# Strassen's seven products in all columns of a down projection, with two weight sums per column made by accumulating loads

## The chip, the cores and the metric

The kernel runs on one core of a Trainium2 chip. The metric is device time in microseconds (us) of one execution. Engines are called as the profile calls them: PE (matrix products; PEld is its weight load), DVE (VectorE), ACT (ScalarE), POOL (GpSimd), SP (SyncE, which only issues DMAs here). All of them run their own instructions in the order in which the program wrote them.

## The reference, cut to what matters

One encoder block on 256 positions with 2048 features, in float32. The last part, in which the change lies, is the feed-forward half:

```python
def _conv_ffn(h, w_up, dw_w, dw_b, w_down):
    up = h @ w_up                                   # 2048 -> 2 x 5504
    gate, val = up[..., :D_FF], up[..., D_FF:]
    gate = conv_general_dilated(gate, dw_w, ...) + dw_b   # width 3, along the positions
    act = jax.nn.gelu(gate, approximate=False) * val
    return act @ w_down                             # 5504 -> 2048
```

Ahead of it stand a norm, an input projection, attention and a Fourier mixing, an output projection and a second norm; behind it the residual sum and a last norm.

## The kernel before, in words

**Operands in two parts.** Every matrix operand is split into a high part in a reduced float32 format (`hi`, a copy by ACT) and the rest (`lo`, a subtraction by DVE, lines 162 and 163, 894 and 895). A product of two such operands is hi x hi + hi x lo + lo x hi on PE. Weights come in tiles of 128 x 2048 numbers (1 MB), by DMAs that SP issues.

**Items.** The 5504 inner features are 43 tiles of 128. PE's work from the second norm on is a list of items (`ff_items`, line 62). An *up item*, `gate` or `val` of one tile, is 16 pairs of matmuls. Tiles 0 to 31 form four groups of eight; a group's down projection runs while the up items of the next group go on. `PATTERN` (line 59) gives the order of a group's items: u is an up item, d a plain down item, s a product. The eleven tiles from 32 on are multiplied afterwards (`down` and `last`).

**The group's down projection.** A group's activations are 1024 features by 256 positions, cut into 2 x 2 blocks (two halves of the features k, two of the positions t). The output columns are four blocks of 512. For the blocks 1 and 3 it is done plainly: four *plain items* with the weight blocks a, c, b, d, of 24 matmuls each (two position halves, 12 each). For the blocks 0 and 2 it is done by Strassen's scheme in Winograd's form: seven *products* P1, N5, N3, P7, P6, P2, N4 of 12 matmuls in place of eight. Their left operands are blocks of activations or sums of them (`operand`, `operand_sums`, lines 857 to 871); their right operands are weight blocks or sums of them: a, x = a+b, d, b+d, x+d, c, x+c. These four sums are DVE additions of 128 x 2048 (lines 912, 920, 927, 936) in the tile `sumw` or in b's own buffer. Each product is added to one or two outputs (`product_out`), and what several outputs share is gathered in three tiles `z_U`, `z_N5`, `z_P7`, and given out once after the last group (`shared_out`, lines 1012 to 1019).

**What sets the order.** Line by line, `ff_step(n)` (line 960) runs after PE's item n was written: first what is noted `beside` n (for the item before: copies and additions out of PSUM, the convolution, the product with the gate), then `split_item(n+2)`, the split of the weights of the item after next, and if the item is an up item one of the `pending` weight sums, then what is noted `behind` n (the GELU, the operands). So ACT and DVE have two items of lead over PE at most; `hi` and `lo` have three buffers each. The weights of the down projection come through a ring of two buffers (`ring_load`, line 880). The operands of the next group are noted at fixed distances after the group's last val item (lines 979 to 985).

**Late tiles.** The up items that go with group 3 are those of the tiles 32 to 39. Their activations are not gathered for a group but split at once (`val_mult`, lines 830 to 833): DVE multiplies, ACT makes the high half, DVE the low half.

Of the kernel before, what the change touches and what calls it, by code (L numbers as in the profile page):

```python
# [8 lines left out]
F32 = mybir.dt.float32  # L9
# [4 lines left out]
P = 128  # L14
# [44 lines left out]
PATTERN = "uuududdudsuusuusuusuusususu"  # L59


def ff_items():
# [20 lines left out]
def block_kernel(  # L83
# [36 lines left out]
    for n, it in enumerate(items):  # L120
        if it[0] in ("product", "plain"):
            continue
# [698 lines left out]
    def val_mult(j):  # L821
        va, ge = sums_of.pop(f"v{j}"), gate_out.pop(j)
        g, q = divmod(j, 8)
        if j >= 8 * N_GROUPS:
            if q % 2 == 0 or j == LAST[0]:
                tag = ("va", "va", "op_P1", "op_A10", "op_P7", "op_N5")[(j - 32) // 2]
# [23 lines left out]
    PLACE = {"P1": (0, 0), "A10": (0, 1), "P2": (1, 0), "N4": (1, 1)}  # L850
# [14 lines left out]
    def operand_sums(g):  # L865
        a00, a10, a01, a11 = (block_of(g, n) for n in ("P1", "A10", "P2", "N4"))
# [11 lines left out]
    ring_next = [0]  # L878

    def ring_load():  # L880
        if ring_next[0] < len(ring):
            key = ring[ring_next[0]]
            ring_next[0] += 1
            t = ring_tiles[key] = fp.tile([P, 2048], F32, tag="rawd", name="rawd%s%d%s" % key)
            col = 0 if key[0] == "s" else 1
            nc.sync.dma_start(t, w_down[(key[1] * 2 + col) * 4 + "abcd".index(key[2])])
# [3 lines left out]
    def two_parts(key, src):  # L890
        hi = wp.tile([P, 2048], F32R, tag="hi", name=f"hi_{key}", bufs=3)
        lo = wp.tile([P, 2048], F32R, tag="lo", name=f"lo_{key}", bufs=3)
        halves[key] = (hi, lo)
        nc.scalar.activation(hi, src, AF.Copy)
        nc.vector.tensor_tensor(lo, src, f32(hi), ALU.subtract)

    def split_product(g, p):
        key = ("product", g, p)
        name = f"{p}_{g}"
        tt = nc.vector.tensor_tensor  # L900
        raw = {w: ring_tiles.get(("s", g, w)) for w in "abcd"}

        def parts_of(src):
            two_parts(name, src)
            halves[key] = halves.pop(name)

        if p == "P1":
            parts_of(raw["a"])
            x = ring_tiles["x"] = fp.tile([P, 2048], F32, tag="sumw", name=f"sumw{g}", bufs=1)
# [6 lines left out]
        elif p in ("N5", "P6", "N4"):  # L916
            parts_of(ring_tiles["x"])
        elif p == "N3":
            parts_of(raw["d"])
# [381 lines left out]
```

## Time and profile before

| | |
|---|---|
| median of 3 runs | 980.5 us (979.66 to 981.6) |
| the profiled execution | 980.02 us, span 978.2 us, mean granted PE clock 0.996 |
| busy: PE, DVE, ACT, POOL | 968.0, 741.8, 516.7, 23.6 us |
| matmuls in one group of items | 180 in plain items and products, 512 in up items |
| moved by DMA | 186.41 MB |
| a weight tile of 1 MB from HBM, from issue to landing | 4.8 us (median) |

In the profile a row of a timeline gives the start, the duration, the engine, the line, the operation, what it writes and reads, and in brackets how long the engine was idle just before and what released it. A matmul's duration covers its way through the array, and the next starts long before its end; so PE's pace is read from start to start. A DVE instruction too starts some 0.08 us before the one ahead of it ends.

### The profile page before, as it was taken

To read this page: it belongs to the slowest core of one execution; us is meant where nothing else is said; L and a number is where in the kernel's file an instruction comes from. 1 tells how busy PE (TensorE), PEld (TensorE's weight loads), DVE (VectorE), ACT (ScalarE), POOL (GpSimd) and SP (SyncE) were. 2 spreads that over 40 slices of the span, in tenths; PEclk is the share of its full clock that TensorE was granted. 3 is DMA by queue.
4 is the path that set the end of the run, shared out by engine and by line. 5 is a ranking of instruction groups with operands and counts; after the bars stand their busy time and mean duration, and the time that the engine had idled before them with its cause. 6 is when DMAs were issued, how large, how long until landed. Compare 5 with 4: busy or idle time off the path is not lost.

```text
span 978.2 us, 12804 instructions
## 1 busy us (share of the span) xinstructions
PE 968.0 (99%) x5137; PEld 829.7 (85%) x5137; DVE 741.8 (76%) x923; ACT 516.7 (53%) x645; POOL 23.6 (2%) x35
## 2 busy tenths in 40 slices
PE   9999999999999999999999999999999999999996
PEld 7788898888888888888888888888888888888885
DVE  6658877576666668787887888778888878887765
ACT  6756766554454455455455455545555545543534
POOL 0000000000000000000000000000000000000003
PEclk9999999999999999999999999999999999999998
DMA  9854444445545755445554464645546544555532
GB/s 328 330 192 145 166 142 160 148 164 208 195 171 190 262 192 191 172 173 216 215 184 172 166 253 166 222 172 179 208 192 217 194 173 144 200 205 211 188 129 86
DMA packets 30091, 186.41 MB, mean 191 GB/s; under 512 B 3408, under 2 KB 3920, under 8 KB 9040
## 3 DMA queue, kind: packets, MB, share of 16 engines
q1 hardware_dynamic: 29744, 184.54, 51.9%
q8 instruction: 40, 0.66, 0.3%
q0 software_dynamic: 144, 1.05, 0.3%
q14 instruction: 19, 0.16, 0.0%
q10 hardware_dynamic: 144, 0.01, 0.0%
HBM read 183.49 MB, written 2.10 MB: 190 GB/s over the span
## 4 chain that ended last, share of the span: by engine, by line
PE 93%; DVE 4%; ACT 2%; DMA 1%; issue 0%; SPq 0%; POOL 0%; ACTq 0%; POOLq 0%
PE ps_val L312 15%; PE ps_gate L312 15%; PE ps_val L313 8%; PE ps_gate L313 8%; PE ps_q L312 5%; PE ps_q L313 2%; PE ps_a L303 2%; PE ps_a L302 2%; PE ps_a L301 2%; DVE lo L163 2%; PE ps_k L312 2%; PE ps_l L302 1%; PE ps_l L301 1%; PE ps_l L303 1%; PE ps_P L1028 1%; PE ps_P L1027 1%
## 5 line engine op out<-in xcount | busy, mean ns | idle before, releaser
L163 DVE TENSOR_TENSOR lo<-raw,hi 128x2048 fp32r<-128x2048 f32 (+3 forms) x146 | 315.3, 2159 | 90.1 <-ACT hi L162 90.0
L162 ACT ACTIVATE hi<-raw 128x2048 fp32r<-128x2048 f32 (+3 forms) x145 | 263.0, 1814 | 62.3 <-PE ps_l L302 18.4
L312 PE MATMUL ps_val<-hU,hi 128*128 128x512 f32 x688 | 242.9, 394 | 0.0
L312 PE MATMUL ps_gate<-hU,hi 128*128 128x512 f32 x688 | 242.8, 394 | 0.0
L313 PE MATMUL ps_val<-hU,lo 128*128 128x256 f32 x688 | 193.1, 281 | 0.1
L313 PE MATMUL ps_gate<-hU,lo 128*128 128x256 f32 x688 | 193.1, 281 | 0.0
L312 PEld LDWEIGHTS ps_gate<-hU,hi 128*128 128x128 f32 x688 | 129.4, 188 | 30.1
L312 PEld LDWEIGHTS ps_val<-hU,hi 128*128 128x128 f32 x688 | 129.4, 188 | 29.9
L313 PEld LDWEIGHTS ps_val<-hU,lo 128*128 128x128 f32 x688 | 128.9, 187 | 1.6 <-DVE lo L163 0.5
L313 PEld LDWEIGHTS ps_gate<-hU,lo 128*128 128x128 f32 x688 | 128.9, 187 | 0.4
L797 ACT ACTIVATE ft_g<-ps_gate 128x256 f32<-128x256 f32 x43 | 16.5, 384 | 105.6 <-PE ps_gate L313 105.6
L797 ACT ACTIVATE ft_v<-ps_val 128x256 f32<-128x256 f32 x43 | 16.6, 385 | 102.0 <-PE ps_val L313 102.0
L312 PE MATMUL ps_q<-hT,hi 128*128 128x512 f32 x192 | 68.5, 397 | 0.0
L313 PE MATMUL ps_q<-hT,lo 128*128 128x256 f32 x192 | 54.0, 281 | 0.0
L312 PEld LDWEIGHTS ps_q<-hT,hi 128*128 128x128 f32 x192 | 36.1, 188 | 8.0
L799 DVE TENSOR_TENSOR fa_g<-ps_gate,ft_g 128x256 f32<-128x256 f32 x43 | 18.1, 422 | 26.7 <-ACT ft_g L797 26.7
L301 PE MATMUL ps_a<-hi,cat 128*128 128x512 f32 x96 | 37.8, 394 | 0.0
L303 PE MATMUL ps_a<-lo,cat 128*128 128x512 f32 x96 | 37.5, 390 | 0.0
L302 PE MATMUL ps_a<-hi,cat 128*128 128x512 f32 x96 | 37.4, 389 | 0.0
L313 PEld LDWEIGHTS ps_q<-hT,lo 128*128 128x128 f32 x192 | 36.1, 188 | 0.0
L799 DVE TENSOR_TENSOR fa_v<-ps_val,ft_v 128x256 f32<-128x256 f32 x43 | 18.2, 423 | 16.0 <-ACT ft_v L797 16.0
L818 ACT ACTIVATE cv<-cv 128x256 f32<-128x256 f32 x43 | 17.8, 415 | 23.4 <-DVE cv L811 23.4
(529 smaller groups left out, 1646.7 us busy)
## 6 DMA issues: line engine op xcount, KB each, us to landing
raw<-in_w_up SPq DMA_DIRECT2D x86, 1024.0 KB, 4.8
raw<-in_w_in SPq DMA_DIRECT2D x21, 1024.0 KB, 5.1
raw<-in_w_out SPq DMA_DIRECT2D x16, 1024.0 KB, 4.8
raw<-in_w_down_late SPq DMA_DIRECT2D x8, 1024.0 KB, 5.0
raw<-in_w_down_last SPq DMA_DIRECT2D x4, 768.0 KB, 4.1
raw<-in_w_in SPq DMA_DIRECT2D x8, 256.0 KB, 5.9
xs<-in_x SPq DMA_DIRECT2D x4, 512.0 KB, 11.1
out_y<-y SPq DMA_DIRECT2D x8, 256.0 KB, 2.5
```

The lines of the kernel that those rows point to most:

```text
L162: nc.scalar.activation(hi[:, s], raw[:, s], AF.Copy)
L163: nc.vector.tensor_tensor(lo[:, s], raw[:, s], f32(hi[:, s]), ALU.subtract)
L301: nc.tensor.matmul(ps, ah, wh, start=first and q == q0, stop=False)
L302: nc.tensor.matmul(ps, al, wh, start=False, stop=False)
L303: nc.tensor.matmul(ps, ah, wl, start=False, stop=last and q == q0 + len(kk) - 1)
L312: nc.tensor.matmul(ps, hi[:, s], h, start=k == 0, stop=False)
L313: nc.tensor.matmul(ps[:, 0:S], lo[:, s], h[:, 0:S], start=False, stop=k == NK - 1)
L797: nc.scalar.activation(tmp, ps[:, S : 2 * S], AF.Copy)
L799: nc.vector.tensor_tensor(add, ps[:, 0:S], tmp, ALU.add)
L818: nc.scalar.activation(cv, cv, AF.Gelu)
L1027: nc.tensor.matmul(ps, o[:, 1, p, :], hi[:, s], start=False, stop=False)
L1028: nc.tensor.matmul(ps, o[:, 0, p, :], lo[:, s], start=False, stop=end)
```

## The change

All four column blocks are now done by the seven products: per group and per c in (0, 1), where c = 0 gives the blocks 0 and 2 and c = 1 the blocks 1 and 3. The plain items go, and with them the operand `A10` that only they used. A group is 14 products of 12 matmuls (168) in place of 4 plain items and 7 products (180). The order of its items is "uuu", then thirteen times "su", then "s". The sums a+b and b+d stay on DVE. The sums x+d and x+c are made by DMAs that POOL issues: they load d, and later c, once more from HBM and add it to `sumw` as it lands. The ring keeps its two buffers; the shared tiles `z` exist once for each c. `shared_out` for c = 0 comes after that column's last product, in the middle of group 3.

```diff
-PATTERN = "uuududdudsuusuusuusuusususu"
+PATTERN = "uuu" + "su" * 13 + "s"
...
-            "d": [("plain", g, w) for w in "acbd"],
-            "s": [("product", g, p) for p in PRODUCTS],
+            "s": [("product", g, c, p) for c in range(2) for p in PRODUCTS],
...
-    ring, ring_tiles = [], {}
-    for g in range(N_GROUPS):
-        ring += [("p", g, w) for w in "acbd"] + [("s", g, w) for w in "abdc"]
+    ring, ring_tiles = [(g, c, w) for g in range(N_GROUPS) for c in range(2) for w in "abdc"], {}
...
+    def split_product(g, c, p):
+
+        raw = {w: ring_tiles.get((g, c, w)) for w in "abcd"}
+        tt = nc.vector.tensor_tensor
+        if p == "P1":
+            ring_tiles["x"] = fp.tile(
+                [P, 2048], F32, tag="sumw", name=f"sumw{g}{c}", bufs=1
+            )
+        x = ring_tiles["x"]
+        src = {"P1": raw["a"], "N3": raw["d"], "P7": raw["b"], "P2": raw["c"]}.get(p, x)
+        hi = wp.tile([P, 2048], F32R, tag="hi", name=f"hi_{p}_{g}{c}", bufs=3)
+        lo = wp.tile([P, 2048], F32R, tag="lo", name=f"lo_{p}_{g}{c}", bufs=3)
+        halves["product", g, c, p] = (hi, lo)
         nc.scalar.activation(hi, src, AF.Copy)
-        nc.vector.tensor_tensor(lo, src, f32(hi), ALU.subtract)
+        tt(lo, src, f32(hi), ALU.subtract)
         if p == "P1":
-            parts_of(raw["a"])
-            x = ring_tiles["x"] = fp.tile([P, 2048], F32, tag="sumw", name=f"sumw{g}", bufs=1)
             def add():
                 tt(x, raw["a"], raw["b"], ALU.add)
                 ring_load()
 
             pending.append(add)
-        elif p in ("N5", "P6", "N4"):
-            parts_of(ring_tiles["x"])
+        elif p == "N5":
+            nc.gpsimd.dma_start(x, weights_of(g, c, "d"), accum_op=ALU.add)
         elif p == "N3":
             pending.append(lambda: tt(raw["b"], raw["b"], raw["d"], ALU.add))
         elif p == "P7":
-            parts_of(raw["b"])
             ring_load()
-            x = ring_tiles["x"]
-
-            def add():
-                tt(x, x, raw["d"], ALU.add)
-                ring_load()
-
-            pending.append(add)
+            ring_load()
+        elif p == "P6":
+            nc.gpsimd.dma_start(x, weights_of(g, c, "c"), accum_op=ALU.add)
+        elif p == "P2":
+            ring_load()
...
-                for m, p in ((2, "P1"), (2, "A10"), (3, "P2"), (3, "N4")):
+                for m, p in ((2, "P1"), (3, "N4"), (3, "P2")):
                     at(behind, n + m, operand, g, p)
                 at(behind, n + 4, operand_sums, g)
                 for m, p in enumerate(("N5", "N3", "P7", "P6")):
                     at(behind, n + 5 + m, operand, g, p)
...
-    def shared_out():
+    def shared_out(c):
...
-        if kind == "product":
...
+        if it[0] == "product":
+            kind, g, c, p = it
+            ps = bank(dn, f"ps_{p}{g}{c}")
+            by_parts(ps, parts[p], *halves.pop(it))
+            at(beside, n + 1, product_out, g, c, p, ps)
             if g == N_GROUPS - 1 and p == PRODUCTS[-1]:
-                at(behind, n + 1, shared_out)
-        elif kind == "plain":
...
+                at(behind, n + 1, shared_out, c)
```

What this moves on DVE, at three places. In the rows the number behind an underscore tells tiles of one name apart, `lo60` is the low part of the weight tile numbered 60 (an up item’s), `fa` and `cv` belong to up items, and `lo_N5_00` is that of product N5 of group 0 and c = 0.

DVE before, at the start of group 0: from the split of the plain item c to the operand of product N5.

```order
L895 TENSOR_TENSOR lo_c_0_3474<-rawdp0c_3095,hi_c_0_3473 128x2048
L868 TENSOR_TENSOR va0k1_3082<-va0k0_2747,va0k1_3082 128x4x128
L869 TENSOR_TENSOR va0k0_2747<-va0k0_2747 128x4x128
L870 TENSOR_TENSOR va0k0_2747<-va0k1_3082,va0k0_2747 128x4x128
L871 TENSOR_TENSOR va0k1_3082<-va0k0_2747,va0k1_3082 128x4x128
L808 SCALAR_TENSOR_TENSOR cv9_3516<-fa_g9_3470,vec_75,cv9_3516 128x255
L811 SCALAR_TENSOR_TENSOR cv9_3516<-fa_g9_3470,vec_75,cv9_3516 128x255
L895 TENSOR_TENSOR lo_b_0_3521<-rawdp0b_3377,hi_b_0_3520 128x2048
L862 TENSOR_TENSOR op_N5_3526<-va0k1_3082,op_N5_3526 128x512
```

DVE now, at the same place.

```order
L903 TENSOR_TENSOR lo_N5_00_3463<-sumw00_3376,hi_N5_00_3462 128x2048
L867 TENSOR_TENSOR va0k1_3085<-va0k0_2750,va0k1_3085 128x4x128
L868 TENSOR_TENSOR va0k0_2750<-va0k0_2750 128x4x128
L869 TENSOR_TENSOR va0k0_2750<-va0k1_3085,va0k0_2750 128x4x128
L870 TENSOR_TENSOR va0k1_3085<-va0k0_2750,va0k1_3085 128x4x128
L807 SCALAR_TENSOR_TENSOR cv9_3504<-fa_g9_3459,vec_75,cv9_3504 128x255
L810 SCALAR_TENSOR_TENSOR cv9_3504<-fa_g9_3459,vec_75,cv9_3504 128x255
L972 TENSOR_TENSOR xs0_92<-ps_P100_3442,xs0_92 128x512
L162 TENSOR_TENSOR lo60_3511<-raw60_3286,hi60_3510 128x2048
L861 TENSOR_TENSOR op_N5_3516<-va0k1_3085,op_N5_3516 128x512
```

The splits of plain items c and b have become those of product N5 and of an up item, and the addition of P1's output stands ahead of the operand. Before, PE came to product N5 seven items after item c; now it comes to N5 right after the up item during which this operand is made.

DVE before, in group 3, from the split of product P2 to that of N4.

```order
L895 TENSOR_TENSOR lo_P2_3_7318<-rawds3c_7133,hi_P2_3_7317 128x2048
L808 SCALAR_TENSOR_TENSOR cv38_7354<-fa_g38_7314,vec_75,cv38_7354 128x255
L811 SCALAR_TENSOR_TENSOR cv38_7354<-fa_g38_7314,vec_75,cv38_7354 128x255
L998 TENSOR_TENSOR z_U_2495<-ps_P63_7296,z_U_2495 128x512
L163 TENSOR_TENSOR lo118_7360<-raw118_7178,hi118_7359 128x2048
L936 TENSOR_TENSOR sumw3_6797<-sumw3_6797,rawds3c_7133 128x2048
L799 TENSOR_TENSOR fa_v38_7382<-ps_val38_7321,ft_v38_7380 128x256
L800 TENSOR_TENSOR fa_v38_7382<-fa_v38_7382,r2b_2494 128x256
L895 TENSOR_TENSOR lo_N4_3_7386<-sumw3_6797,hi_N4_3_7385 128x2048
```

DVE now, at the same products of c = 1 in group 3.

```order
L903 TENSOR_TENSOR lo_P2_31_7413<-rawd31c_7281,hi_P2_31_7412 128x2048
L829 TENSOR_TENSOR fa_v38_7409<-fa_v38_7409,cv38_7382 128x256
L832 TENSOR_TENSOR act_38_7449<-fa_v38_7409,act_38_7449 128x256
L978 TENSOR_TENSOR z_U1_2498<-ps_P631_7394,z_U1_2498 128x512
L162 TENSOR_TENSOR lo119_7455<-raw119_7255,hi119_7454 128x2048
L798 TENSOR_TENSOR fa_g39_7475<-ps_gate39_7416,ft_g39_7473 128x256
L799 TENSOR_TENSOR fa_g39_7475<-fa_g39_7475,r2b_2494 128x256
L903 TENSOR_TENSOR lo_N4_31_7479<-sumw31_7064,hi_N4_31_7478 128x2048
```

The addition of c to `sumw` is gone from DVE, and an up item's activation (a val of the late tiles, then a gate) has moved into the place.

DVE before, behind the last product of group 3.

```order
L163 TENSOR_TENSOR lo121_7496<-raw121_7363,hi121_7495 128x2048
L1014 TENSOR_TENSOR z_N5_2496<-z_N5_2496,z_U_2495 128x512
L1015 TENSOR_TENSOR xs2_94<-xs2_94,z_N5_2496 128x512
L1016 TENSOR_TENSOR z_N5_2496<-z_N5_2496,z_P7_2497 128x512
L1017 TENSOR_TENSOR xs2_94<-xs2_94,z_N5_2496 128x512
L1018 TENSOR_TENSOR z_U_2495<-z_U_2495,z_P7_2497 128x512
L1019 TENSOR_TENSOR xs0_92<-xs0_92,z_U_2495 128x512
```

DVE now, between the sum a+b and the split of N5 for c = 1 of group 3.

```order
L907 TENSOR_TENSOR sumw31_7064<-rawd31a_6798,rawd31b_6934 128x2048
L995 TENSOR_TENSOR z_N50_2496<-z_N50_2496,z_U0_2495 128x512
L996 TENSOR_TENSOR xs2_94<-xs2_94,z_N50_2496 128x512
L997 TENSOR_TENSOR z_N50_2496<-z_N50_2496,z_P70_2497 128x512
L998 TENSOR_TENSOR xs2_94<-xs2_94,z_N50_2496 128x512
L999 TENSOR_TENSOR z_U0_2495<-z_U0_2495,z_P70_2497 128x512
L1000 TENSOR_TENSOR xs0_92<-xs0_92,z_U0_2495 128x512
L798 TENSOR_TENSOR fa_v36_7138<-ps_val36_7069,ft_v36_7136 128x256
L799 TENSOR_TENSOR fa_v36_7138<-fa_v36_7138,r2b_2494 128x256
L903 TENSOR_TENSOR lo_N5_31_7142<-sumw31_7064,hi_N5_31_7141 128x2048
```

Six additions that stood behind the group's last product now stand, for c = 0, between two of its splits; those for c = 1 still stand at the end.

More of the change, by code (lines that the diff above doesn't have):

```diff
@@ L865, in operand_sums @@
     def operand_sums(g):
-        a00, a10, a01, a11 = (block_of(g, n) for n in ("P1", "A10", "P2", "N4"))
+        a00, a10, a01, a11 = (block_of(g, n) for n in ("P1", "P7", "P2", "N4"))
         tt = nc.vector.tensor_tensor
@@ L985, in up_posts, with to_out @@
                     at(behind, n + 5 + m, operand, g, p)
[L988 to L991 removed]
+    Z = {}
+    for c in range(2):
+        for z in ("U", "N5", "P7"):
+            pool, tag = (wp, "junk") if (c, z) == (1, "P7") else (fp, f"z_{z}{c}")
+            Z[c, z] = pool.tile([P, 512], F32, tag=tag, name=f"z_{z}{c}", bufs=1)
+    def to_out(c, n, t, ps):
+        xb = xs[2 * n + c][:, t, :]
         nc.vector.tensor_tensor(xb, ps, xb, ALU.add)
@@ L1021, in by_parts @@
-    def by_parts(ps, o, hi, lo, first, last):
+        u, n5, p7 = (Z[c, z] for z in ("U", "N5", "P7"))
+        tt(n5, n5, u, ALU.subtract)
+        tt(xs[2 + c][:, 0, :], xs[2 + c][:, 0, :], n5, ALU.add)
+        tt(n5, n5, p7, ALU.subtract)
+        tt(xs[2 + c][:, 1, :], xs[2 + c][:, 1, :], n5, ALU.add)
+        tt(u, u, p7, ALU.add)
+        tt(xs[c][:, 1, :], xs[c][:, 1, :], u, ALU.add)
+    def by_parts(ps, o, hi, lo):
         for p in range(4):
             s = slice(p * 512, (p + 1) * 512)
-            end = last and p == 3
-            nc.tensor.matmul(ps, o[:, 0, p, :], hi[:, s], start=first and p == 0, stop=False)
+            nc.tensor.matmul(ps, o[:, 0, p, :], hi[:, s], start=p == 0, stop=False)
```

92 lines of the change are left out of this document (23 added, 69 removed).

## The prediction

> **What bounds the kernel now.** I read the page first (busy shares, then the chain that ended last), then busy time in windows cut at the first product of each of the four groups, then PE and VectorE (DVE) instruction by instruction at the place where the change begins, and last the DMA issues.
>
> ```profile
> span 978.2 us, 12804 instructions
> PE 968.0 (99%) x5137; PEld 829.7 (85%) x5137; DVE 741.8 (76%) x923; ACT 516.7 (53%) x645; POOL 23.6 (2%) x35
> PE 93%; DVE 4%; ACT 2%; DMA 1%; issue 0%; SPq 0%; POOL 0%; ACTq 0%; POOLq 0%
> ```
>
> PE has work throughout and carries 93% of the chain. The windows show the stage that the change touches. Their columns are the window, its length, then the busy time and instruction count of PE, weight loads, DVE, ACT and POOL, the granted clock, the DMA share and GB/s.
>
> ```profile
> 370.47:500.87 130.40, 130.40 (x695) 112.03 (x693) 105.47 (x109) 68.70 (x70) 0.00 (x0) 1.00 0.53 194
> 500.87:631.28 130.41, 130.41 (x694) 112.02 (x693) 107.18 (x112) 67.05 (x67) 0.00 (x0) 1.00 0.53 194
> 631.28:761.69 130.41, 130.41 (x694) 112.03 (x693) 107.19 (x112) 67.05 (x67) 0.00 (x0) 1.00 0.53 194
> 761.69:875.70 114.01, 113.94 (x598) 97.28 (x597) 95.94 (x103) 59.76 (x62) 0.74 (x1) 1.00 0.50 179
> ```
>
> PE is busy in the whole of every window at a granted clock of 1.00. DVE is busy for 107.2 of 130.4 us, 82%, and for 95.9 of 114.0, 84%, in the last. ACT needs about half. So PE is the bound, DVE has about 23 us of room in a group, and the DMA engines are half used. The question is whether DVE's room outlasts what the change hands it.
>
> **The change, part by part.** *Matmuls.* These PE rows give the length of each kind of item, from first matmul to first matmul of the next.
>
> ```profile
> 500.87 0.39 PE L1026 MATMUL ps_d1a<-hi_a,op_P 128*128 128x512 f32 x1
> 506.33 0.40 PE L312 MATMUL ps_val<-hU,hi 128*128 128x512 f32 x1
> 542.19 0.39 PE L312 MATMUL ps_gate<-hU,hi 128*128 128x512 f32 x1
> 547.77 0.39 PE L1026 MATMUL ps_N<-hi_N,op_N 128*128 128x512 f32 x1
> 550.52 0.40 PE L312 MATMUL ps_val<-hU,hi 128*128 128x512 f32 x1
> ```
>
> A plain item of 24 matmuls takes 506.33 - 500.87 = 5.46 us, an up item 547.77 - 542.19 = 5.58, a product of 12 matmuls 550.52 - 547.77 = 2.75. A group loses 4 plain items (21.84) and gains 7 products (19.25): 2.6 us. By matmuls it is 12 x 5.46/24 = 2.73. Four groups give 10.4 to 10.9; I take **10.7 us** off PE. A group is then 16 x 5.58 + 14 x 2.75 = 127.8 us of PE.
>
> *DVE, per group.* Splits into two parts go from 11 to 14, products' and plain items' additions to outputs from 12 to 16, the operand A10 goes, and the weight sums on DVE stay at four (a+b and b+d for each of two columns; before, all four of one column). The rows below show 2.29 us for a split, 0.69 for an operand, 0.68 for an output. Added: 3 x 2.29 + 4 x 0.68 - 0.69 = 8.9 us. That makes 107.2 + 8.9 = 116.1 of 127.8 us, 91%. On the average it fits; the sums that the accumulating loads take over would be 4 x 2.29 = 9.2 us more. But DVE works in a fixed order and splits only two items ahead, so a group is decided by its densest stretch.
>
> *The start of group 0.* This is DVE in the kernel before, from the split of the up item that follows the third of the group (start, duration, instruction, idle before it). The PE row gives the start of that third item.
>
> ```profile
> 364.81 0.40 PE L312 MATMUL ps_gate<-hU,hi 128*128 128x512 f32 x1
> ```
>
> ```profile
> 367.30 2.29 DVE L163 TENSOR_TENSOR lo<-raw,hi 128x2048 fp32r<-128x2048 f32 x1 [0.51 <-ACT hi L162]
> 369.50 0.69 DVE L862 TENSOR_TENSOR op_P<-va0k,op_P 128x512 fp32r<-128x512 f32 x1
> 370.11 0.69 DVE L862 TENSOR_TENSOR op_N<-va0k,op_N 128x512 fp32r<-128x512 f32 x1
> 370.71 0.42 DVE L839 TENSOR_TENSOR va1k<-fa_v,cv 128x256 f32<-128x256 f32 x1
> 371.08 0.42 DVE L799 TENSOR_TENSOR fa_g<-ps_gate,ft_g 128x256 f32<-128x256 f32 x1
> 371.54 0.42 DVE L800 TENSOR_TENSOR fa_g<-fa_g,r2b 128x256 f32<-128x256 f32 x1
> 372.89 2.29 DVE L895 TENSOR_TENSOR lo_c<-rawdp0c,hi_c 128x2048 fp32r<-128x2048 f32 x1 [0.92 <-ACT hi_c L894]
> 375.10 0.68 DVE L868 TENSOR_TENSOR va0k<-va0k,va0k 128x512 f32<-128x512 f32 x1
> 375.81 0.69 DVE L869 TENSOR_TENSOR va0k<-va0k 128x512 f32<-128x512 f32 x1
> 376.54 0.69 DVE L870 TENSOR_TENSOR va0k<-va0k,va0k 128x512 f32<-128x512 f32 x1
> 377.26 0.69 DVE L871 TENSOR_TENSOR va0k<-va0k,va0k 128x512 f32<-128x512 f32 x1
> 377.87 0.48 DVE L808 SCALAR_TENSOR_TENSOR cv<-fa_g,vec,cv 128x255 f32<-128x255 f32 x1
> 378.39 0.49 DVE L811 SCALAR_TENSOR_TENSOR cv<-fa_g,vec,cv 128x255 f32<-128x255 f32 x1
> 378.79 2.29 DVE L895 TENSOR_TENSOR lo_b<-rawdp0b,hi_b 128x2048 fp32r<-128x2048 f32 x1
> 380.99 0.69 DVE L862 TENSOR_TENSOR op_N<-va0k,op_N 128x512 fp32r<-128x512 f32 x1
> ```
>
> The last row makes operand N5. Before, product N5 came eight items later, and nobody waited. Now it is the sixth item of the group, and the same 15 instructions stand ahead of its operand, with splits of other items in their slots, plus the sum a+b (one 2.20 step, as from 367.30 to 369.50) and the addition of P1's output (a 0.60 step). From the first row to the operand's end it was 380.99 + 0.69 - 367.30 = 14.38 us; now 14.38 + 2.20 + 0.60 - 0.92 (the wait for hi_c, covered) = 16.26. The stretch starts 367.30 - 364.81 = 2.49 us after PE starts the third up item, so the operand is done 18.75 us after that. PE comes to N5 after up, P1, up: 5.58 + 2.75 + 5.58 = 13.91. PE waits 4.8 us, less 0.2 because the first matmul reads only the half that ACT makes: **4.6 us**.
>
> *Groups 1 and 2.* There the previous group ends with a product, and all operands stand one step earlier against PE. The first late thing is the split of the up item behind N5. From that of the up item behind P1, in steps of the rows above: split 2.21, sum 2.20, operand sums 0.71 + 0.73 + 0.72 + 0.61, product with the gate 0.37, two scaled sums 0.46 + 0.42, split of N5 2.20, operand 0.61, convolution 0.52 + 0.40, two outputs 1.20, split 2.29: 15.65 us. With the 2.49 it ends 18.1 us after PE starts the third up item; PE can begin its second matmul after 5.58 + 2.75 + 5.58 + 2.75 + 0.23 = 16.89. Wait: 1.2. The next eighteen DVE steps, which hold the sum b+d and three operands, come to 17.6 us against 16.7 of PE, 1.0 more. As a bound from below, DVE may lead by some tenths at each place; I take **2.0 us a group**, 1.2 to 2.4.
>
> *Group 3.* Here the up items are those of the late tiles, whose values DVE and ACT hand to and fro.
>
> ```profile
> 865.19 0.42 DVE L830 TENSOR_TENSOR fa_v<-fa_v,cv 128x256 f32<-128x256 f32 x1
> 866.09 0.42 DVE L833 TENSOR_TENSOR act<-fa_v,act 128x256 fp32r<-128x256 f32 x1 [0.48 <-ACT act L832]
> 866.43 0.68 DVE L992 TENSOR_TENSOR xs<-ps_P,xs 128x512 f32<-128x512 f32 x1
> 867.89 2.29 DVE L163 TENSOR_TENSOR lo<-raw,hi 128x2048 fp32r<-128x2048 f32 x1 [0.78 <-ACT hi L162]
> ...
> 876.82 0.68 DVE L1014 TENSOR_TENSOR z_N<-z_N,z_U 128x512 f32<-128x512 f32 x1
> ...
> 880.31 0.69 DVE L1019 TENSOR_TENSOR xs<-xs,z_U 128x512 f32<-128x512 f32 x1
> ```
>
> DVE waits 0.48 for ACT's half and 0.78 for the split that ACT starts after it, 1.26 per val item. The six additions that end the products (876.82 to 881.00, 4.2 us) lay behind the last product; for the first column they now stand in the middle of the group. DVE from the first product to the late items: 95.9 + 8.9 + 4.2 = 109.0 busy, with 7 x 1.26 = 8.8 of waits 117.8 us; PE has 14 x 2.75 + 13 x 5.58 = 111.0. That is 6.8 us short; where some 0.4 of ACT lag stays in each of the gate pairs too, 10. I take **8.5 us**.
>
> *The accumulating loads.* None is in the trace. DVE hands `sumw` to POOL after the split of N5 and of P6, and ACT wants it back for P6 and N4. The second is the tighter: product pairs follow each other every 2.75 + 5.58 = 8.33 us, so ACT comes to N4 16.7 us after it began P6, and 4.2 of that go to the two halves of P6's split: 12.5 us are left, 11.2 where DVE is a further 1.3 late. Behind ACT's wait there would stand the splits of all later items. The nearest rows (issuing engine, KB, us to landing, and the busy share of the loads' queue):
>
> ```profile
> gfb<-in_normf_g POOLq DMA_DIRECT2D x1, 1024.0 KB, 5.1
> raw<-in_w_up SPq DMA_DIRECT2D x86, 1024.0 KB, 4.8
> xs<-in_x SPq DMA_DIRECT2D x4, 512.0 KB, 11.1
> q1 hardware_dynamic: 29744, 184.54, 51.9%
> 865.96 0.74 POOL L1146 DMA_DIRECT2D gfb<-in_normf_g  x1 [594.85 <-DVE fa_v L830]
> ```
>
> A POOL load of the same size landed in 5.1 us; the queue's share, 0.519 x 978.2 / 184.54, gives 2.9 us of all engines per 1.05 MB. An addition on the way must read the old sum as well: a second pass, 5.1 + 2.9 = 8.0 us (an estimate). The ends are 5.1 and, by the slowest landing here, 11.1 or somewhat more; I take 8, hidden by the 11.2, at no cost. [...] The engines' extra 4 x 5.8 us per group bring their share from 0.53 to about 0.73: other loads stay hidden.
>
> **Sum.** -10.7 + 4.6 + 2 x 2.0 + 8.5 = +6.4 us. The profiled execution took 980.0 us for its span of 978.2; that becomes 986.4, and from the median of the runs, 980.5, **986.9, say 987 us**.
>
> **Rivals.** *Faster: PE stays the bound.* DVE's 91% fits on the average; if what I count as waits closes up, the 10.7 us remain: 970 us. For it speaks that a before with 82 to 84% never stops PE for long; against it, that the N5 operand has no slack in the order itself. With half of my waits (8.5 us) it would be 978. *Slower still: the accumulating load lands late.* It decides from some 12 us on (11.2 and about 1 before PE is reached); each further us is paid at eight N4 products, 8 us per us: 14 us make 1001, 16 us 1017. For it, the 11.1 row and that both reads run on the engines that feed everything else; against it, the 5.1 row. *About no change:* waits of 10.7 us in all cancel the gain, 980.
>
> **How the numbers follow.** A measurement here tells 0.2% (2 us) from no change. DVE's order as counted: 0.70, 983 to 991. Late landing: 0.17, from 991 up. PE stays the bound, in whole or in half: 0.09. Cancelled: 0.04. So slower 0.87, same 0.04, faster 0.09. The range takes 979 to 1000: below it lies most of the faster case, above it landings past 14 us, about 2 in 10 together.
>
> **What would show it.** Right: PE idle ahead of the first N5 by 4 to 5 us, released by DVE's operand; short PE waits for `lo` at the starts of groups 1 and 2 and many in group 3; DVE without idle time there; landings under 11 us. Wrong: PE gapless from 370 on (then my DVE count is), or ACT waiting for `sumw` from a DMA (then the landing is).

## The result, and the profile after

| | before | after |
|---|---|---|
| median (lowest to highest) | 980.4 us (979.66 to 981.6, 4 runs) | 993.2 us (992.23 to 993.49, 4 runs) |
| ratio to before, 95% interval | | 1.0128 (1.011 to 1.0145) |
| span of the profiled execution | 978.2 us | 991.6 us |

The change makes the kernel 12.8 us slower; forecast were 6.4 (987, range 979 to 1000). "Page" below is the page of the profile. Of the page of after: the span, the busy times, and the shares of the chain that ended last.

```profile
span 991.6 us, 12783 instructions
PE 964.7 (97%) x5089; PEld 822.0 (83%) x5089; DVE 775.4 (78%) x950; ACT 537.8 (54%) x656; POOL 37.4 (4%) x51
PE 80%; DVE 14%; ACT 3%; issue 2%; DMA 1%; SPq 0%; POOL 0%; ACTq 0%; POOLq 0%
```

DVE's share of the chain went from 4 to 14 per cent, PE's from 93 to 80. Now the windows, cut at the first product of each group, here of groups 0, 1 and 3, with the columns as in the prediction.

```profile
371.79:506.35 134.56, 130.26 (x682) 111.39 (x681) 112.69 (x114) 75.37 (x75) 3.66 (x4) 0.97 0.67 219
506.35:636.43 130.08, 128.46 (x682) 109.66 (x681) 114.88 (x118) 72.10 (x69) 3.47 (x4) 1.00 0.69 227
...
766.45:888.07 121.62, 113.55 (x586) 94.58 (x585) 106.98 (x116) 65.45 (x66) 4.06 (x5) 1.00 0.66 211
```

Groups 1 and 2 (2 is like 1) take 130.1 and 130.0 us, before 130.4, though a group has 2.7 us less to multiply: nearly all of the saving is eaten. Group 0 takes 134.6 (before 130.4) and group 3 121.6 (before 114.0): there the kernel gets slower. What PE waits for between 370 and 905 us, in total, times, longest:

```profile
PE ps_N L1007 <- DVE op_N L861: 5.6, 2, 4.3
PE ps_gate L312 <- DVE lo L162: 5.5, 6, 1.3
PE ps_val L312 <- DVE lo L162: 3.5, 3, 1.8
PE ps_l L300 <- DVE xs L1013: 0.7, 1, 0.7
...
PE ps_P L1008 <- DVE lo_P L903: 0.5, 1, 0.5
```

Every wait is for DVE, none for a DMA, and ACT waits for no accumulating load. The longest stands ahead of the first N5 of group 0. PE there, and then DVE:

```profile
380.11 0.39 PE L1006 MATMUL ps_N<-hi_N,op_N 128*128 128x512 f32 x1
384.79 0.80 PE L1007 MATMUL ps_N<-hi_N,op_N 128*128 128x512 f32 x1 [4.30 <-DVE op_N L861]
385.38 0.63 PE L1008 MATMUL ps_N<-lo_N,op_N 128*128 128x512 f32 x1
385.81 0.63 PE L1006 MATMUL ps_N<-hi_N,op_N 128*128 128x512 f32 x1
...
389.56 0.39 PE L311 MATMUL ps_gate<-hU,hi 128*128 128x512 f32 x1
```

```profile
381.86 2.28 DVE L162 TENSOR_TENSOR lo<-raw,hi 128x2048 fp32r<-128x2048 f32 x1
384.05 0.68 DVE L861 TENSOR_TENSOR op_N<-va0k,op_N 128x512 fp32r<-128x512 f32 x1
```

This is the order that the prediction counted: split of the up item, then operand of N5. DVE has no gap, and PE loses 384.79 - 380.11 - 0.23 = 4.45 us. What the prediction did not have is the rest of the first fence: after the wait the matmuls start 0.43 us apart (385.38, 385.81) instead of 0.23, nearly to the end of N5. N5 takes 389.56 - 380.11 = 9.45 us, of which 2.75 are its work, 4.45 the wait and 2.25 the slow pace. The same stretch as a window:

```profile
384.79:389.60 4.81, 4.81 (x12) 3.81 (x13) 3.84 (x5) 0.00 (x0) 0.00 (x0) 0.52 0.74 257
```

The granted clock is 0.52 in it: it stood at 0.50 from 382.62 us, in the middle of the wait, to 389.44. In group 3, `shared_out` for c = 0 and a late tile's val stand between the splits (DVE, then PE):

```profile
836.31 0.69 DVE L1000 TENSOR_TENSOR xs<-xs,z_U 128x512 f32<-128x512 f32 x1
...
837.71 2.28 DVE L903 TENSOR_TENSOR lo_N<-sumw,hi_N 128x2048 fp32r<-128x2048 f32 x1
...
840.88 0.42 DVE L832 TENSOR_TENSOR act<-fa_v,act 128x256 fp32r<-128x256 f32 x1 [0.54 <-ACT act L831]
...
842.68 2.29 DVE L162 TENSOR_TENSOR lo<-raw,hi 128x2048 fp32r<-128x2048 f32 x1 [0.18 <-ACT hi L161]
```

```profile
845.03 0.39 PE L312 MATMUL ps_val<-hU,lo 128*128 128x256 f32 x1 [1.83 <-DVE lo L162]
```

PE waits for the split of N5 and then 2.1 us for that of the up item. The accumulating loads, from issue to landing (median), beside the one plain load that POOL issues:

```profile
sumw<-in_w_down POOLq DMA_DIRECT2D x16, 1024.0 KB, 8.4
gfb<-in_normf_g POOLq DMA_DIRECT2D x1, 1024.0 KB, 5.0
```

They landed after 8.0 to 9.9 us; 8.0 was the estimate.

### The profile page after: what moved, and what is told of

It is laid out like the page before. It is cut to its first block, busy times and chain, and to the rows that moved or that the text cites. A ratio compares the mean times of both kernels' runs of the same rounds, so it can differ in the third digit from the quotient of the medians.

```text
span 991.6 us, 12783 instructions
## 1 busy us (share of the span) xinstructions
PE 964.7 (97%) x5089; PEld 822.0 (83%) x5089; DVE 775.4 (78%) x950; ACT 537.8 (54%) x656; POOL 37.4 (4%) x51
## 3 DMA queue, kind: packets, MB, share of 16 engines
q1 hardware_dynamic: 29744, 184.54, 50.6%
## 4 chain that ended last, share of the span: by engine, by line
PE 80%; DVE 14%; ACT 3%; issue 2%; DMA 1%; SPq 0%; POOL 0%; ACTq 0%; POOLq 0%
PE ps_val L311 13%; PE ps_gate L311 13%; PE ps_gate L312 7%; PE ps_val L312 6%; PE ps_q L311 5%; DVE lo L162 4%; PE ps_q L312 2%; PE ps_a L302 2%; PE ps_a L300 2%; PE ps_a L301 2%; PE ps_P L1006 2%; PE ps_P L1008 2%; PE ps_P L1007 2%; DVE lo_N L903 2%; PE ps_k L311 2%
## 5 line engine op out<-in xcount | busy, mean ns | idle before, releaser
L1008 PE MATMUL ps_P<-lo_P,op_P 128*128 128x512 f32 x128 | 50.2, 392 | 0.5 <-DVE lo_P L903 0.5
L1006 PE MATMUL ps_P<-hi_P,op_P 128*128 128x512 f32 x128 | 50.2, 392 | 0.0
L1007 PE MATMUL ps_P<-hi_P,op_P 128*128 128x512 f32 x128 | 49.8, 389 | 0.0
L903 DVE TENSOR_TENSOR lo_N<-sumw,hi_N 128x2048 fp32r<-128x2048 f32 x16 | 36.6, 2290 | 11.1 <-ACT hi_N L902 11.1
L1007 PE MATMUL ps_N<-hi_N,op_N 128*128 128x512 f32 x96 | 38.6, 402 | 5.6 <-DVE op_N L861 5.6
L1008 PE MATMUL ps_N<-lo_N,op_N 128*128 128x512 f32 x96 | 38.5, 401 | 0.5 <-DVE lo_N L903 0.5
L1006 PE MATMUL ps_N<-hi_N,op_N 128*128 128x512 f32 x96 | 38.3, 399 | 0.0
```

The costliest lines, as they stand in the source:

```text
L903: tt(lo, src, f32(hi), ALU.subtract)
L1006: nc.tensor.matmul(ps, o[:, 0, p, :], hi[:, s], start=p == 0, stop=False)
L1007: nc.tensor.matmul(ps, o[:, 1, p, :], hi[:, s], start=False, stop=False)
L1008: nc.tensor.matmul(ps, o[:, 0, p, :], lo[:, s], start=False, stop=p == 3)
```

## The experiments

The theory: DVE's fixed order, two items ahead of PE, makes PE wait where much DVE work stands together (start of a group, b+d, `shared_out`); the accumulating loads cost nothing. The main rival: the loads cost the time. A second: DVE is too full, and moving work within its order gains nothing. Where an expectation speaks of a walk through the queues, each instruction is started when its engine and its operands are free, with the durations of the rows shown. "After" below is 993.2 us; each experiment ran beside the kernel before on its own chip (981.3, 980.9, 980.8 and 980.7 us in the four sessions).

**e1, no accumulating loads.**

```diff
         elif p == "N5":
-            nc.gpsimd.dma_start(x, weights_of(g, c, "d"), accum_op=ALU.add)
...
         elif p == "P6":
-            nc.gpsimd.dma_start(x, weights_of(g, c, "c"), accum_op=ALU.add)
```

> The changed kernel with the two accumulating loads of every column left out (so x+d and x+c are not made, and the products P6 and N4 multiply a+b instead); DVE, ACT, PE and SP do the same instructions as before the edit. Theory (DVE's fixed order makes PE wait; the accumulating loads land in time): no change, 992 to 994 us, the same PE waits, 4.4 us ahead of the first N5. Rival (the accumulating loads cost the time, by landing late or by slowing other loads on the 16 engines): a good part of the 12.8 us comes back, 980 to 988 us.

Measured: 992.7 us, ratio to before 1.0121 (1.0107 to 1.0134). The longest wait is the same:

```profile
PE ps_N L1003 <- DVE op_N L861: 5.6, 2, 4.3
```

Taking 16 MB out of the traffic and the adding with it gives nothing back: 0.5 us, less than runs of one kernel differ by (992.2 to 993.5 in after). The rival falls.

**e4, the loads alone, in the kernel before.**

```diff
-                tt(x, x, raw["d"], ALU.add)
-                tt(x, x, raw["c"], ALU.add)
+            if p != "N4":
+                w = w_down[g * 8 + (3 if p == "N5" else 2)]
+                nc.gpsimd.dma_start(x, w, accum_op=ALU.add)
```

> The kernel before with one part of the change alone: in its one Strassen column per group the sums x+d and x+c are made by accumulating loads that POOL issues, and not by DVE; order of items, products and plain items stay. Theory (the loads land in time and disturb nobody): as the kernel before, 979.5 to 981.5 us, PE gapless in the groups. Rival (an accumulating load costs PE time): eight of them at 0.8 us, half of the 12.8 us of the change, 986 to 987 us.

Measured: 981.2 us, ratio 0.9999 (0.999 to 1.0008). Group 0 in a window from its first plain item on:

```profile
372.24:502.60 130.36, 130.36 (x694) 111.98 (x693) 101.32 (x107) 68.65 (x70) 1.93 (x2) 1.00 0.62 210
```

PE has no gap; DVE has 4.2 us less to do than before (105.5), and nobody gains from that, since PE was the bound. That half of the change is free, and here worth nothing.

**e2, the operands of group 0 one step earlier.**

```diff
+                e = g == 0
-                for m, p in ((2, "P1"), (3, "N4"), (3, "P2")):
+                for m, p in ((2, "P1"), (3 - e, "N4"), (3 - e, "P2")):
...
-                at(behind, n + 4, operand_sums, g)
+                at(behind, n + 4 - e, operand_sums, g)
...
-                    at(behind, n + 5 + m, operand, g, p)
+                    at(behind, n + 5 - e + m, operand, g, p)
```

> The changed kernel with the operands of group 0 made one step earlier (N4, P2, the operand sums, N5, N3, P7 and P6), which puts the operand of N5 ahead of the split of the up item behind P1, as groups 1 to 3 have it. Theory: the 4.4 us stall ahead of the first N5 goes, and with it the slow pace of its 12 matmuls (0.43 for 0.23 us each, 2.3 us); some 0.3 us of waits stay at the next up item: 993.2 - 4.4 - 2.3 + 0.3 = 986.8 us. Rival 1 (the slow pace has another cause than the stall): 989 us, N5 still 2.3 us too long. Rival 2 (DVE is simply too full, and the wait comes back at the next items): 992 to 993 us.

Measured: 987.6 us, ratio 1.0063 (1.0051 to 1.0076). N5 takes 2.74 us, its full pace, and the next up item waits briefly (first row). The second row is a window in group 3, further down:

```profile
383.58 0.39 PE L312 MATMUL ps_gate<-hU,lo 128*128 128x256 f32 x1 [0.35 <-DVE lo L162]
```

```profile
840.12:843.53 3.41, 3.41 (x13) 2.93 (x12) 3.38 (x4) 2.64 (x3) 0.00 (x0) 0.50 0.97 262
```

One step's move is worth 5.6 us: stall and slow pace go together (6.7 us), 0.5 us of wait comes back. The rest is the second row, of the profiled execution: here the clock fell to half behind the wait of 1.82 us (2.10 by starts) in group 3, which in after it did not (1.00 from 843.42 to 850.24 us, around a wait of 1.83). That costs 1.7 us, half of 3.41, and since DVE caught up meanwhile, the wait of 1.35 us that follows in after is missing. e5 has the same stretch (840.60 to 844.02).

**e5, only N5's operand ahead of the split.**

```diff
-                    at(behind, n + 5 + m, operand, g, p)
+                    at(beside if g + m == 0 else behind, n + 5 + m, operand, g, p)
```

> The changed kernel with one instruction pair moved: the operand of group 0's N5 is made ahead of the split of the up item behind P1, not behind it. The stall ahead of N5 falls from 4.4 to about 1.4 us, and the split moved back gives a new wait of 1.7 us at the up item after it: 1.2 us less of waits in all, but in two short ones. Theory (the slow pace of N5's matmuls comes from one long idle time of PE; idle times up to 2.1 us in the trace were followed by the full pace): the slow pace goes too, 2.3 us: 993.2 - 1.2 - 2.3 = 989.7 us, N5's 12 matmuls in 2.75 us. Rival (it comes from any idle time there, or from product N5 itself): 992 us, N5 at 0.43 us a matmul.

Measured: 988.2 us, ratio 1.0075 (1.0062 to 1.0088). PE at N5 and at the up item behind it:

```profile
380.38 0.50 PE L1007 MATMUL ps_N<-hi_N,op_N 128*128 128x512 f32 x1 [0.58 <-DVE op_N L861]
380.72 0.39 PE L1008 MATMUL ps_N<-lo_N,op_N 128*128 128x512 f32 x1
380.95 0.39 PE L1006 MATMUL ps_N<-hi_N,op_N 128*128 128x512 f32 x1
...
384.10 0.39 PE L312 MATMUL ps_gate<-hU,lo 128*128 128x256 f32 x1 [0.68 <-DVE lo L162]
```

Two short waits, 0.7 and 0.9 us, leave the pace at 0.23. So product N5 as such is not slow; the idle time ahead of it made it so. The two waits came out shorter than the walk through the queues had them, hence 988.2 and not 989.7.

**e3, without b+d.**

```diff
-            pending.append(lambda: tt(raw["b"], raw["b"], raw["d"], ALU.add))
+            pass
```

> The changed kernel with the sum b+d left out (P7 multiplies b alone), which takes one 2.2 us step out of DVE's order in each of the eight columns, and nothing else. Theory (DVE's dense stretches): the waits behind N3 and P7 go, 0.77 and 0.82 at the second up item of groups 1 and 2, and in group 3 0.62, 1.06 and 1.35: 4.6 us in all, 988.6 us; the waits ahead of N5 stay. Rival (PE waits for something else than DVE's amount of work): 993 us.

Measured: 988.1 us, ratio 1.0072 (1.0059 to 1.0084). The waits for an up item's split fell from 5.5 us in six (`ps_gate`) and 3.5 in three (`ps_val`) to

```profile
PE ps_gate L312 <- DVE lo L162: 3.3, 3, 1.3
PE ps_val L312 <- DVE lo L162: 2.3, 2, 1.8
```

and the one for `lo_P` is gone: the five waits named in the expectation went, and no other. Of the 8 x 2.2 = 17.6 us of DVE work taken out, only 5 us came back: those places where the order was tight.

**e6, `shared_out` in pairs behind the late down items.**

```diff
-            if g == N_GROUPS - 1 and p == PRODUCTS[-1]:
-                at(behind, n + 1, shared_out, c)
+            if (g, c, p) == (N_GROUPS - 1, 1, PRODUCTS[-1]):
+                for m in range(6):
+                    at(behind, n + 2 + m, shared_out, m % 2, m // 2)
```

> The changed kernel with the twelve additions of shared_out taken out of group 3 and written in pairs behind the late down items. Theory (the 4.2 us of DVE in mid-group hold up the splits of N5 and of the next up item, and the six at the end hold up the outputs of the late stage): the waits of 0.66, 0.25 and 2.10 us around 840 to 847 and 0.86 at 900 go, 3.8 us: 989.4 us; the wait of 1.35 at 863 stays. Rival (another part of DVE's work takes the place): 992 to 993 us.

Measured: 988.7 us, ratio 1.0084 (1.007 to 1.0098). The waits around 840 to 847 and that of the late stage (`ps_l`) are gone, the one behind P7 of c = 1 stays, 1.3 us.

**e8, the same instructions in another order.** e2 and e6 together, and an order for each group that a walk through the queues with the durations of the trace found.

```diff
-PATTERN = "uuu" + "su" * 13 + "s"
+PATTERNS = ['uuuususuusussusussuussuusssuus',
+            'uuuusususuussuusssuussuussuuss',
+            'uuuusususususuusssuususussuuss',
+            'uusususuusususussuusuusussuuss']
...
-        items += [todo[c].pop(0) for c in PATTERN]
+        items += [todo[c].pop(0) for c in PATTERNS[g]]
```

> The changed kernel with the same instructions in another order: the operands of group 0 one step earlier, the additions of shared_out in pairs behind the late down items, and for each group an order of its own in which the up items stand two or more together where DVE has more to do (four ahead of group 0's first product, pairs behind N5 and at the group's end) and products stand in pairs where it has less. Theory (only the places of the dense stretches cost the time; the average DVE load of 91 per cent fits): two us of waits stay, PE is the bound: 993.2 - 22.8 + 2 = 972 us, faster than the kernel before by 8; up to 976 where a wait or two more come up. Rival (DVE at 91 per cent gives the waits back wherever the items stand): 983 to 990 us.

Measured: 974.3 us, ratio 0.9934 (0.992 to 0.9947): 6.6 us faster than the kernel before, 18.9 faster than after. Page, then the waits of PE between 370 and 905 us, then a window in the groups:

```profile
span 970.8 us, 12827 instructions
PE 958.7 (99%) x5089; PEld 821.5 (85%) x5089; DVE 773.9 (80%) x950; ACT 538.6 (55%) x656; POOL 37.5 (4%) x51
```

```profile
PE ps_val L312 <- DVE lo L162: 1.8, 1, 1.8
```

```profile
496.00:626.00 130.00, 130.00 (x694) 111.65 (x693) 118.00 (x122) 73.70 (x72) 3.47 (x4) 1.00 0.68 230
```

In the window PE has no gap in 130 us, with DVE busy for 118.0 of them, 91 per cent. Forecast were 972, and up to 976 where a wait or two more come up; measured were 974.3, 972.6 in the profiled execution. Of all the waits one is left, 2.0 us at a val of group 3. So the second rival falls too: DVE at 91 per cent keeps up where the order spreads its work. e8 is the fastest version, and beats both kernels.

**e7 and e9, the accumulating loads later.** How much room do they have? In e7 POOL multiplies `sumw` by 1.0 ahead of each load; in e9 it multiplies two columns and then writes a small tile of its own 50 times.

```diff
+            nc.gpsimd.tensor_scalar(x, x, 1.0, None, ALU.mult)
```

```diff
+            nc.gpsimd.tensor_scalar(x[:, 0:2], x[:, 0:2], 1.0, None, ALU.mult)
+            for _ in range(50):
+                nc.gpsimd.memset(pause, 0.0)
```

> The changed kernel with a POOL multiplication of sumw by 1.0 ahead of each accumulating load, so that the load begins and lands later by that step's length, which the trace will give (four times the 1.29 us of a POOL product of 128 x 512, 5.2 us, as an estimate: landing 13.6 after DVE's split). Theory (there is room of 11 to 12 us, and behind it ACT waits): up to 2.5 us of delay nothing; at 5.2 us, by a walk through the queues with the durations of the trace, some 4 us: 997 us; by the price of the prediction (8 us for each us past 12): 1006 us; PE then waits ahead of N4, and ACT for a DMA. Rival (the loads have much more room than counted): 993 us still.

> As e7, but what delays the accumulating loads doesn't read a large tile: one POOL multiplication of two numbers per partition of sumw (which waits for DVE's split) and then 50 small memsets of a tile of its own, some 3 to 5 us by the memset rows of the trace (0.04 to 0.1 us from start to start). If the delay is D, the load lands about 8.4 + 0.9 + D after DVE's split. Theory: DVE's instructions keep their lengths (lo 2.29 us, no 5.3 us ones), so that nearly all of e7's 50 us goes; of the late landing itself there stay, by the walk through the queues, some 2 us at D = 4 and 4 us at D = 5: 994 to 998 us; by the price in the prediction (8 us for each us past 12) up to 1010 us. Rival (in e7 it was the late landing that cost the 50 us): 1020 us or more.

Measured: e7 1043.7 us, ratio 1.0642 (1.0627 to 1.0656); e9 1048.6, ratio 1.0696 (1.0675 to 1.0717). Both missed, for reasons of their own. In e7 the delay was not all: POOL and DVE of that kernel show

```profile
377.39 5.59 POOL L912 TENSOR_SCALAR sumw<-sumw 128x2048 f32<-128x2048 f32 x1 [105.45 <-DMA rawd00d<-in_w_down]
```

```profile
377.78 4.02 DVE L868 TENSOR_TENSOR va0k<-va0k 128x512 f32<-128x512 f32 x1
...
412.17 5.32 DVE L162 TENSOR_TENSOR lo<-raw,hi 128x2048 fp32r<-128x2048 f32 x1 [0.33 <-ACT hi L161]
```

DVE instructions of 0.69 and 2.29 us took 4.02 and 5.32 beside POOL's step; DVE's busy time rose from 775.4 to 820.7 us. So e7 measures two things, and no run parts them. Its loads landed 17.0 us after DVE's split of P6 in the mean; by the price found below that would be some 20 to 25 of its 50 us (an estimate). In e9 DVE's instructions kept their lengths (773.9 us busy), but the memsets took 9.0 us, not 3 to 5, so it tells of a landing far outside the room.

**e11 and e12, 20 and 10 memsets.**

> As e9 with 20 memsets in place of 50. By the rows of e9 (0.25 and 0.44 us for the POOL multiplication, 0.18 a memset, 9.1 from issue to landing) the load lands 0.7 + 3.6 + 9.0 = 13.3 us after DVE's split. By the price of the prediction, 8 us for each us past 12: 993 + 10 = 1003 us; by the walk through the queues 997 us; with more room than counted 993 us.

> As e9 with 10 memsets: landing 0.7 + 1.8 + 8.8 = 11.3 us after DVE's split, 3 us later than in the changed kernel, still inside the counted room of 12. Theory: no change that can be told, 992 to 995 us. Rival (the room is smaller than counted, and the changed kernel stood at its edge): 998 us or more.

Measured: e11 1007.6 us, ratio 1.0271 (1.0256 to 1.0287); e12 998.0, ratio 1.0176 (1.0159 to 1.0193). What ACT waits for, in e12, e11 and e9:

```profile
ACT hi_N L903 <- DMA sumw<-in_w_down: 0.6, 1, 0.6
```

```profile
ACT hi_N L903 <- DMA sumw<-in_w_down: 27.1, 8, 5.4
```

```profile
ACT hi_N L903 <- DMA sumw<-in_w_down: 65.5, 8, 10.5
```

By its number e12 fits the rival (998 us or more), but not for the rival's reason. ACT comes once to a sum that is not there, by 0.6 us, at 12.2 us after DVE's split of P6, and PE's waits are no longer than in after (by some 3 us shorter in all). So its 4.8 us over after are not lateness; about 1 us of them is more work at half clock (6.8 us against 4.7). What grew else is the length of PE's matmuls: the same group of PE rows, in after and in e12 (busy, mean ns of one).

```profile
L1008 PE MATMUL ps_P<-lo_P,op_P 128*128 128x512 f32 x128 | 50.2, 392 | 0.5 <-DVE lo_P L903 0.5
```

```profile
L1015 PE MATMUL ps_P<-lo_P,op_P 128*128 128x512 f32 x128 | 50.7, 396 | 0.5 <-DVE lo_P L904 0.5
```

From start to start the products' matmuls take 233 ns in e9, e11 and e12 and 229 in all others, e10 on e9's chip among them. These three have the small tile `pause` (128 bytes a partition) and POOL's memsets in common; which of them slows PE, if either does, wasn't tried.

So e12 is the base for the other two. How late the sum is can be read from DVE's split of P6 and the start of ACT's next use of the sum, here in e11 in group 1:

```profile
538.71 2.29 DVE L904 TENSOR_TENSOR lo_P<-sumw,hi_P 128x2048 fp32r<-128x2048 f32 x1
```

```profile
557.48 1.92 ACT L903 ACTIVATE hi_N<-sumw 128x2048 fp32r<-128x2048 f32 x1 [4.93 <-DMA sumw<-in_w_down]
```

That is 557.48 - 538.71 - 2.29 = 16.5 us. Over the eight N4 it is 13.1 to 17.4 in e11, 15.4 in the mean, at a cost of 1007.6 - 998.0 = 9.6 us; in e9 19.7 in the mean, and 50.6. That is 41.0 / 4.3 = 9.5 us for each us of landing. Of the 41.0 some 12 are slow pace: PE worked 31.9 us at half clock between 360 and 945 us in e9, 8.4 in e11, and loses half of that. Without it 6.8 us are left for each us; the 8 of the prediction lies between. The point from which it decides is then about 15.4 - 9.6/9.5 = 14.4 us, 14.1 with 6.8: some 14 us, not 12 (an estimate from means). In after the loads landed 8.3 to 10.2 us behind the same split, 9.2 in the mean, so the change is about 5 us away from it. e11's 9.6 us over e12 are near the 10 that the price gave, but by two errors that cancel: the loads took 10.8 us from issue to landing in this kernel, not 9.0, and the room is larger. The 1003 us were missed by the slower matmuls.

**e10, idle times of several lengths ahead of N5.**

```diff
-        nc.vector.tensor_tensor(o[:, 1], a, f32(o[:, 0]), ALU.subtract)
+        for _ in range((6, 5, 6, 5)[g] if name == "N5" else 1):
+            nc.vector.tensor_tensor(o[:, 1], a, f32(o[:, 0]), ALU.subtract)
```

> The kernel of e2 with the subtraction of N5's operand done several times over (six times in groups 0 and 2, five in 1 and 3; the same numbers each time), which makes PE wait ahead of N5 once in each group, by the walk through the queues 3.2, 2.4 to 2.7, 3.2 to 3.5 and 4.4 us. It looks for the length of idle time from which PE's pace drops. Theory (a threshold between the 2.1 us that did nothing and the 4.4 us that did): after the 4.4 us of group 3 the 12 matmuls of N5 stand 0.43 us apart for about 5 us, after the 2.4 to 2.7 us of group 1 they stand 0.23 apart; the two of 3.2 to 3.5 us tell on which side of the threshold they lie. Time: 987.6 + 13.1 of waits + 2.3 for each slow stretch: 1003 to 1008 us. Rival (the slow pace was something of group 0's first product alone): all of N5 at 0.23, 1000 to 1001 us.

Measured: 1002.1 us, ratio 1.0213 (1.0196 to 1.023), between the theory's 1003 and the rival's 1001: the waits came out some tenths shorter than forecast. The first matmul after the wait in groups 0, 1, 2 and 3, and in 0 and 2 the next:

```profile
383.35 0.79 PE L1009 MATMUL ps_N<-hi_N,op_N 128*128 128x512 f32 x1 [3.02 <-DVE op_N L862]
383.94 0.63 PE L1010 MATMUL ps_N<-lo_N,op_N 128*128 128x512 f32 x1
...
516.52 0.50 PE L1009 MATMUL ps_N<-hi_N,op_N 128*128 128x512 f32 x1 [2.36 <-DVE op_N L862]
...
650.22 0.50 PE L1009 MATMUL ps_N<-hi_N,op_N 128*128 128x512 f32 x1 [3.08 <-DVE op_N L862]
650.57 0.40 PE L1010 MATMUL ps_N<-lo_N,op_N 128*128 128x512 f32 x1
...
784.99 0.71 PE L1009 MATMUL ps_N<-hi_N,op_N 128*128 128x512 f32 x1 [4.22 <-DVE op_N L862]
```

After 4.22 us the pace dropped, after 2.36 it did not, and of two waits of the same length one (3.02) dropped it and one (3.08) did not. So the rival falls (group 3 is slow too), and the length alone does not decide. What does can be read from the granted clock. In every trace here it is 1.00 or 0.50 and changes only at points that lie multiples of 3.41 us apart, in e10 at 382.33, 389.16, 785.10, 788.52, 853.37 and 856.78. Two neighbouring steps of that length around the wait of 3.08 us, then two around a later wait of 1.83 us at a val item (columns as above):

```profile
648.57:651.98 3.41, 1.76 (x8) 1.44 (x9) 3.31 (x7) 0.80 (x3) 0.00 (x0) 1.00 0.94 192
651.98:655.39 3.41, 2.17 (x11) 1.51 (x10) 3.41 (x4) 3.41 (x3) 0.00 (x0) 1.00 0.38 77
...
849.96:853.37 3.41, 1.68 (x7) 0.83 (x5) 3.23 (x3) 3.29 (x3) 0.00 (x0) 1.00 0.90 159
853.37:856.78 3.41, 3.22 (x10) 2.83 (x11) 3.38 (x5) 2.40 (x2) 0.00 (x0) 0.50 1.00 250
```

The wait of 3.08 us is shared by two steps, 1.43 and 1.65 us of idle time, and the clock stays; the shorter one puts 1.73 us into one step, and the next has half the clock. Over all traces, between 260 and 945 us, each of the 28 steps at full clock with 1.73 us or more of idle time was followed by half clock, and none with 1.65 or less was; the one exception seen lies behind that stretch (1.90 us, e7 at 946). In after it is 2.13 us in the step from 379.21 that half clock follows, and 1.61 in that from 843.42 that it does not. So in these executions 1.73 us of idle time in one step were enough, and where the steps lie against the program changed from one to the next: one begins at 382.62 us in after and at 382.33 in e10.

## Why the prediction was right, and what was off

Direction and mechanism held: PE waits for DVE in the places named, and the accumulating loads cost nothing. The forecast size was half of what came: 6.4 us forecast, 12.8 by the medians, 13.4 by the spans of the profiled executions (991.6 - 978.2). The terms that were missing or too small all have the same sign, so nothing cancelled.

| term | forecast | measured | shown by |
|---|---|---|---|
| matmuls | -10.7 | -10.4 | e8: span 7.4 shorter with 2.0 of wait left and 1.0 of later start |
| group 0, wait at N5 | +4.6 | +4.45 | e2, e5 |
| group 0, pace after it | none | +2.3 | e2, e5, e10 |
| groups 1 and 2 | +2.0 each | +2.0 each (1.18 and 0.8) | e3 takes the 0.8 |
| group 3 | +8.5 (6.8 to 10) | +9.6 in waits over 0.2 us, 10.6 by its length | e3 and e6 take parts |
| late stage | none | +0.95 | e6 |
| accumulating loads | 0 | 0 | e1, e4, e12 |

The measured terms come to -10.4 + 4.45 + 2.3 + 4.0 + 10.6 + 0.95 = +11.9 us. Another 1.3 of the 13.4 lies ahead of the change (the first up item starts at 263.1 us, before at 261.8); e4, whose work there is that of the kernel before, has it at 263.6, and the other runs between 262.1 and 263.9, so this is scatter between executions. 0.2 has no name.

*Group 0.* The step "PE waits 4.8 us, less 0.2" was right to 0.15 us. What failed is that it took the wait as the whole price. A wait of 4.45 us put the granted clock at 0.52 for the next 4.8 us. How long the wait is did not decide it alone: the clock changed at steps of 3.41 us that lie differently against the program in each execution, and 1.73 us idle in one step were enough (e10, and waits of 1.8 us in e1, e2, e5, e11 and e12). The trace of before has the clock at 0.50 in one place, its end, from 971.41 us, 2.1 us after the last matmul; the prediction did not use that, and no matmul ran there that could have shown the pace.

*Groups 1 and 2.* The counted steps gave 1.2 and 1.0; the trace has 1.18 twice, and 0.77 and 0.82.

*Group 3.* The size came out at or a little over the upper end: the val hand-over between DVE and ACT, b+d and `shared_out` each gave the waits foreseen, but the step that failed is the balance of DVE's total (117.8 us) against PE's over the whole group: DVE lags at one place and idles at another, so the waits come to more than the difference of the totals. DVE was busy for 107.0 of the 121.6 us, near the 109.0 reckoned, but idle for 14.6, where the prediction had 8.8. In e8, where the order is another, one wait of 2.0 us is left of this group's 9.6.

*The late stage.* The six additions of c = 1 at the end of the group held up the outputs of the first late item, 0.86 us. Before, six such additions stood there too and PE did not wait; now DVE comes out of the group without a lead, which the prediction did not carry on into the next stage.

*The accumulating loads.* 8.4 us against the estimate of 8.0, and 5.0 for the plain load. That the 3.4 us more are a second pass was the author's estimate; no run here parts the reads from the adding. The room was about 14 us, not 12.

*The rivals.* "PE stays the bound", 970 us, had 0.09, and it fell: the order had no slack, as the prediction said. But by e8 this is a property of the order and not of DVE's load: with the same instructions the median is 974.3 us. "Late landing" would have needed about 5 us more. "Half of the waits close up" did not happen; the counted waits all came, and in group 3 more.

## What to carry over

An engine with 91 per cent of its time used kept up where the order gave it its work evenly (e8: DVE busy for 118.0 of 130 us, PE without a gap); count the densest stretch between two points where the bound engine needs it, and not the average, and before giving up a saving look for a better order of the same instructions (here 18.9 us). Add to a wait of the matrix engine the slow matmuls behind it: here they followed waits of 1.83 us (e10) and 4.30 us (after), and not one of 3.08 us (e10). A resource that a change newly uses (here loads that add) may be the suspicious part and yet free (992.7 us without them, 993.2 with): take it out alone, and put it in alone.

## What the runs showed of the hardware that was not expected

- **Clock after idle time.** After a wait of 4.45 us the granted clock was 0.52 and 128x512 matmuls started 0.43 us apart for 4.8 us (after); after 2.36 us it did not fall (e10), and after 1.83 us in the same execution it did. The clock changed on a grid of 3.41 us; in e10 it fell behind a step with 1.73 us of idle time and not behind one with 1.65.
- **DVE beside POOL's multiplications.** Beside a POOL multiplication of 128x2048 (5.58 and 5.50 us in the mean, at its two places) a DVE `tensor_tensor` took 4.02 us for 0.69 and another 5.32 for 2.29 (e7); beside memsets on POOL (9.0 us at a stretch) none took longer (e9). Over the sixteen multiplications of e7 one DVE instruction each was longer by 2.2 to 3.4 us, and not by all of POOL's 5.5: DVE's busy time rose by 45.3 us, 2.8 for each. Why is not shown.
- **A slower pace of unknown cause.** With a further tile of 128 bytes a partition and POOL's memsets on it, product matmuls took 233 ns for 229 from start to start (e9, e11, e12). The cause stays open.
- **Memsets.** 50 POOL memsets of 128x32 took 9.0 us, 0.18 each.
